# Moving the pieces of the gate weights' sums behind the MLP's first product, and two gate turns into the embedding products

## The chip, the cores and the metric

The kernel runs on one core of one Trainium2 chip. The metric is the time of one execution on the device, in microseconds. The core's engines work side by side, each on its own queue in order: TensorE (PE) multiplies, VectorE (DVE) and ScalarE (ACT) work on tiles element by element, SyncE (SP) issues most of the DMA transfers, and ScalarE's queue issues some as well. They wait for each other through semaphores.

## The reference

Two layers of a decoder trunk on 512 tokens of width 1024, all float32. Each layer is a token mixer (SSD, then HGRN2), a layer norm, an MLP with squared ReLU, a second layer norm and a gated embedding:

```python
def sq_relu_mlp(h, w1, w2):
    a = jax.nn.relu(h @ w1)
    return (a * a) @ w2
...
        h = layer_norm(DEEPNORM_ALPHA * x + mix, ln_g[i, 0], ln_b[i, 0])
        h = layer_norm(DEEPNORM_ALPHA * h + sq_relu_mlp(h, mlp_w1[i], mlp_w2[i]), ln_g[i, 1], ln_b[i, 1])
        x = h + jax.nn.sigmoid(h @ ple_w_gate[i]) * (p[i] @ ple_w_proj[i])
```

The change lies in the last two of these lines: w1 is 1024 x 4096, w2 4096 x 1024, the gate weights 1024 x 1024 and the embedding's projection 256 x 1024.

## The kernel before

**Arithmetic.** Every float32 factor is split into a high and a low part (`split`: a copy to the matmul's type on ScalarE, L114, into a `whi` tile; a subtraction on VectorE, L116, into a `wlo` tile), and `mm3` multiplies three of the four pairs (L120 to L122), 128x128 by 128x512 each. The pools of whi and wlo tiles have six slots each, which all the weights share. A slot that is written again waits for everything that read it.

**The MLP's schedule.** The hidden 4096 columns are worked on in four groups. `hidden(g)` makes a group's 8 tiles of the first product (each a T: 24 matmuls, ReLU L528, square L530); after every four of them `half_blocks` (L345 to L371) makes half of the group's seven blocks a11, a22, a12, s2, s3, s1 and s4, sums and differences of quarters, each put as a high copy (L357, ScalarE) and a low rest (L358, VectorE). The blocks s3 and s4 live in `blk` buffers, of which there are two per name, the others in `b8` buffers. `block_product` then makes the group's part of the second product in seven products p1 to p7 of 24 matmuls (each a Q), from these blocks and from sums of w2's quarters; every product is added to `acc` on VectorE (L471, or L473 the first time, L467 in the last group). The table `PERIODS` sets the order: period 0 is eight Ts, periods 1 to 3 are TTQTQTQTQTQTQTQ (the Ts of group g, the Qs of group g - 1), period 4 is seven Qs. The first Q of a period is p1 (a11).

**The gate weights' sums.** The gate's product uses the same scheme, so its weights' sums are made ahead: `sums_ahead` (L392 to L425) is a generator of 20 steps. For each of four pieces it takes one whi and one wlo tile as room for four quarters (loads L402 on SP), makes the sums (L405, L406, then L409, L410 on VectorE), and then, in two pairs, copies the high part into an `sg` tile (L417) and stores it to `pre` in memory (L418), subtracts to get the low part (L420, VectorE), and stores that (L425, issued by ScalarE). The whi and wlo slots are held until the last L425 has landed. `sg` has two buffers. The period loop takes one step after each Q of periods 1 to 3; what is left is taken at the start of period 4.

**Order.** The schedule follows the order in which the program is written, with offsets of priority, and `behind(x)` keeps what is issued within it behind the instruction x. The vector rows of the gate pieces stand behind `marks["acc"]`, the last accumulate that was written (L467, L471 or L473); the L425 stores stand behind `marks["act"]`, the last ReLU.

**Turns and embedding.** After the MLP, `turned(c)` transposes a chunk of the normed rows on TensorE (L318, into banks pt and pm) and splits it for the gate's product. turned(0) stands behind the last matmul of p3 in period 4 (c, k = 1, 3), turned(1) between proj(0, 0) and proj(1, 0), which are the first two products of the embedding (6 matmuls each).

Of the kernel before, what the change touches and what calls it, by code (L numbers as in the profile page):

```python
# [16 lines left out]
T = 512  # L17
# [15 lines left out]
SUMS = (60, 300, 300, 300)  # L33
# [8 lines left out]
def trunk(ctx: ExitStack, tc, a):  # L42
    nc = tc.nc
# [14 lines left out]
    uid, marks = [0], {}  # L58
# [5 lines left out]
    def mk(p, shape, tag, dt=F32, **kw):  # L64
        return p.tile(list(shape), dt, tag=tag, name=nm(tag), **kw)

    def f32(t):
        return t.bitcast(F32)
# [21 lines left out]
    def bank(p, tag):  # L90
        return mk(p, [P, T], tag)
# [8 lines left out]
    def behind(ins):  # L100
        return nullcontext() if ins is None else tc.issue_after(ins.ins)
# [17 lines left out]
    def mm3(out, sh, sl, mh, ml, start, stop, **kw):  # L119
        nc.tensor.matmul(out, sh, mh, start=start, stop=False, **kw)  # L120
        nc.tensor.matmul(out, sh, ml, start=False, stop=False, **kw)  # L121
        marks["pe"] = nc.tensor.matmul(out, sl, mh, start=False, stop=stop, **kw)  # L122
# [25 lines left out]
    acc = mk(accp, [P, NCH, D], "acc")  # L148
# [10 lines left out]
    with tc.high_priority(offset=FIRST):  # L159
# [7 lines left out]
        for k in range(8):  # L167
            hi, lo = (v[:, k % 4, :] for v in early[k // 4])
            x, w = slots[k][:, 0:T], slots[k][:, T:768]
# [180 lines left out]
    def half_blocks(blk, z0, z1, p):  # L350

        ks = slice(2 * p, 2 * p + 2)
        a11, a12, a21, a22 = z0[:, :, 256:], z1[:, :, 256:], z0[:, :, :256], z1[:, :, :256]

        def put(name, f):
            hi, lo = blk[name][:, 0, ks, :], blk[name][:, 1, ks, :]
            nc.scalar.copy(hi, f)  # L357
            nc.vector.tensor_sub(lo, f, f32(hi))  # L358

        put("a11", a11)  # L360
        put("a22", a22)
        nc.vector.tensor_add(a22, a21, a22)
        put("a12", a12)
        nc.vector.tensor_sub(a21, a11, a21)
        nc.vector.tensor_sub(a11, a22, a11)
        nc.vector.tensor_sub(a12, a12, a11)
        put("s2", a11)
        put("s3", a21)
        put("s1", a22)
        put("s4", a12)  # L370
# [65 lines left out]
            us.append((hi, lo))  # L436
        return us

    def block_product(w, blk, lead, first, after=None, turns=None, sums=None):

        with behind(marks.pop(("turned", 0), None) if first else None):
            t1, t2, t3, t4 = weight_sums(w, lead)
        seen = set() if first else {(i, j) for i in range(2) for j in range(2)}
        banks = {}

        def product(x, f, name, start, i, j, turns=None):
            us = [split(v) if f in (t1, t2, t3, t4) else unit(v) for v in f]
            if start:  # L450
                banks[name] = [bank(psy, "py%d" % c) if name == "x" else bank(psj, "pj") for c in range(2)]
            t = blk[x]
            for c in range(2):
                ps = banks[name][c]
                sl = slice(c * P, (c + 1) * P)
                for k in range(4):
                    hi, lo = us[k // 2]
                    ks = slice((k % 2) * 512, (k % 2 + 1) * 512)
                    w_ = hi[:, ks], lo[:, ks]
                    mm3(ps, t[:, 0, k, sl], t[:, 1, k, sl], *w_, start and k == 0, k == 3, skip_group_check=True)  # L460
                    if turns and (c, k) == (1, 3):
                        with behind(marks["pe"]):
                            turns()
                d = acc[:, 2 - 2 * i + c, j * 512 : (j + 1) * 512]
                with tc.high_priority(offset=SOON if after else 0):
                    if after and f in (w[1][0], t1, t4, w[1][1]):
                        marks["acc"] = nc.vector.tensor_tensor_reduce(  # L467
                            d, ps, d, 1.0, 0.0, ALU.add, ALU.add, sums[:, 2 - 2 * i + c, j : j + 1]
                        )
                    elif (i, j) in seen:  # L470
                        marks["acc"] = nc.vector.tensor_add(d, ps, d)  # L471
                    else:
                        marks["acc"] = nc.vector.scalar_tensor_tensor(d, d, ALPHA, ps, ALU.mult, ALU.add)  # L473
            seen.add((i, j))

        p1 = lambda: product("a11", w[0][0], "x", True, 0, 0)
        p2 = lambda: product("a12", w[1][0], "z", True, 0, 0)
        p6 = lambda: product("s2", t2, "x", False, 1, 0)
        p7 = lambda: product("s3", t3, "y", True, 1, 1)
        p5 = lambda: product("s1", t1, "x", False, 1, 1)  # L480
        p4 = lambda: product("a22", t4, "y", False, 1, 0)
        p3 = lambda: product("s4", w[1][1], "x", False, 0, 1, turns)
        for f in (p1, p7, p6, p4, p5, p2, p3) if after else (p1, p2, p6, p7, p5, p4, p3):
            f()
            if after and f is p5:
                after(0), after(1)
            if after and f is p3:
                after(2), after(3)
            yield

    def mlp_and_gate(layer, h_s, last, turns=()):

        w1, w2 = a[f"w1_{layer}"], a[f"w2_{layer}"]
        blocks = {}
# [45 lines left out]
        for g, period in enumerate(PERIODS):  # L540
            if g < 4:
                tiles = hidden(g)
            if g > 0:
                if g == 4:
                    blk, after, turned, sums, later = norm_blocks(2 * layer + 1)
                    p_s = (mk(w4, [P, 2, T], "a", F32R), mk(w4, [P, 2, T], "b", F32R))
                    praw = mk(raws, [P, 1024], "raw")
                    nc.sync.dma_start(praw, a[f"pT_{layer}"].rearrange("p k t -> p (k t)"))
                    praw = praw.rearrange("p (k t) -> p k t", k=2)
                    nc.scalar.copy(p_s[0], praw)  # L550
                    nc.vector.tensor_sub(p_s[1], praw, f32(p_s[0]))
                w = [[[w2[8 * g - 8 + 4 * i + 2 * j + u] for u in range(2)] for j in range(2)] for i in range(2)]
                products = block_product(w, blocks.pop(g - 1), SUMS[g - 1], g == 1, *((after, lambda: turned(0), sums) if g == 4 else ()))
            for op in period:
                next(tiles if op == "T" else products)
                if 0 < g < 4 and op == "Q":
                    next(ahead, None)
                if g == 4:
                    for _ in ahead:
                        pass  # L560
# [14 lines left out]

        pus, pps, held = {}, {}, {}

        def proj(c, h, parts=1):
            if h not in pus:
                pus[h] = unit(a[f"wp_{layer}"][h])  # L580
            pu = pus[h]
            pps[c, h] = []
            n = 512 // parts
            for i in range(parts):
                pp = bank(psj, "pj")[:, :n]
                for k in range(2):
                    ks = slice(k * 512 + i * n, k * 512 + (i + 1) * n)
                    mm3(pp, p_s[0][:, k, c * P : (c + 1) * P], p_s[1][:, k, c * P : (c + 1) * P], pu[0][:, ks], pu[1][:, ks], k == 0, k == 1)
                pps[c, h].append(pp)

        def product(x, f, c, ps, start, hook=()):
            cs = slice(c * P, (c + 1) * P)
            for k in range(4):
                hi, lo = f[k // 2]
                ks = slice((k % 2) * 512, (k % 2 + 1) * 512)
                mm3(ps, blk[x][:, 0, k, cs], blk[x][:, 1, k, cs], hi[:, ks], lo[:, ks], start and k == 0, k == 3, skip_group_check=True)
                for at in hook:
                    if (c, k) == at[:2]:
                        with behind(marks["pe"]):
                            turned(at[2])  # L600
# [15 lines left out]
                late.append(lambda: turn(h, c))  # L616

        two = lambda p, tag: [bank(p, tag % c if "%" in tag else tag) for c in range(2)]
        proj(0, 0)
        with behind(marks["pe"]):  # L620
            turned(1)
        proj(1, 0)
        xb = two(psy, "py%d")
        f = [unit(v) for v in wb[0][0]]
        for c in range(2):
# [3 lines left out]
        f = [unit(v) for v in wb[1][0]]  # L629
# [8 lines left out]
        f = ready(pre, 2)  # L638
# [9 lines left out]
        f = ready(pre, 1)  # L648
# [4 lines left out]
        f = ready(pre, 3)  # L653
# [5 lines left out]
        f = ready(pre, 0)  # L659
# [7 lines left out]
        f = [unit(v) for v in wb[1][1]]  # L667
# [14 lines left out]
    first = [bank(psy, "py0"), bank(psy, "py1")]  # L682
    for k in range(8):
        if k == 6:
            for i in range(8):
                for c in range(NCH):
# [4 lines left out]
                        start=i == 0,  # L691
# [3 lines left out]
        parts = [tuple(v[:, k % 4, i * P : (i + 1) * P] for v in early[k // 4]) for i in range(2)]  # L695
# [241 lines left out]
    with tc.manual_schedule(engines={mybir.EngineType.PE}):  # L937
# [8 lines left out]
        for k in range(1, 9):  # L946
            i, j = 2 * k, 2 * k + 1
# [542 lines left out]
```

## Time and profile before

| | us |
|---|---|
| median of 3 runs (1411.07 to 1411.56) | 1411.1 |
| the profiled execution | 1411.54 |
| its span, first to last instruction | 1409.8 |
| ScalarE busy in it | 777.6 |
| VectorE busy in it | 1076.0 |

The first layer's MLP runs from about 393 to 700 us of the span, the second layer's about 652 us later. Times in rows are microseconds from the start of the span. A row of the timeline gives the start, the duration, the engine, the line, the operation and the tiles (written<-read, buffer numbers left out), and in brackets the idle time of the engine before it with what ended it. A queue's name with a q (ACTq, SPq) is the engine issuing a DMA.

### The profile page before, as it was taken

The page shows a single profiled execution, that of the slowest core. Times are in us where ns is not written, and L with a number is a line of the kernel's source. Part 1 is how long each engine was busy: PE and PEld are TensorE (multiplying, and loading weights), DVE is VectorE, ACT ScalarE, POOL GpSimd, SP SyncE. Part 2 cuts the span into 40 slices and gives each one's busy share as a digit, 9 for nine tenths or more (in the row PEclk, how much of TensorE's full clock was granted, in tenths as well). Part 3 has the DMA queues.
Part 4 walks back from the last instruction along what each step waited for, and adds up shares of the span by engine and source line. Part 5 has one row for each costly group of instructions (what it writes and reads, how often), then busy time and mean ns, then how long its engine had stood idle before and what let it go on. Part 6 is the DMA issues. An engine that isn't in the chain of part 4 may idle for free.

```text
span 1409.8 us, 20492 instructions
## 1 busy us (share of the span) xinstructions
PE 1400.4 (99%) x7973; PEld 1168.9 (83%) x7973; DVE 1076.0 (76%) x1777; ACT 777.6 (55%) x1164; POOL 1.8 (0%) x11
## 2 busy tenths in 40 slices
PE   9999999999999999999999999999999999999998
PEld 7888888888988888887888888888898888888787
DVE  7997877696866878787985774776785877868986
ACT  7886666573554555545564446465454554544563
POOL 0000000000000000000000000000000000000000
PEclk9999999999999999999999999999999999999999
DMA  8423333323354646655473321222163566565364
GB/s 295 157 98 135 103 108 120 105 90 105 129 185 143 228 161 204 211 176 177 139 280 122 104 92 62 89 92 75 61 239 122 171 209 214 175 215 194 108 246 154
DMA packets 66819, 214.70 MB, mean 152 GB/s; under 512 B 7713, under 2 KB 8353, under 8 KB 66593
## 3 DMA queue, kind: packets, MB, share of 16 engines
q1 hardware_dynamic: 57504, 196.59, 41.6%
q10 hardware_dynamic: 9216, 16.78, 3.3%
q8 instruction: 63, 1.03, 0.3%
q14 instruction: 36, 0.29, 0.1%
HBM read 194.41 MB, written 18.94 MB: 151 GB/s over the span
## 4 chain that ended last, share of the span: by engine, by line
PE 96%; DMA 1%; DVE 1%; ACT 1%; issue 1%; SPq 0%; DVEq 0%; ACTq 0%
PE pj L120 25%; PE pj L122 24%; PE pj L121 24%; PE py L120 5%; PE py L122 5%; PE py L121 5%; PE py L881 1%; PE py L1147 1%; PE py L883 1%; DVE wlo L116 1%; PE pt L864 0%; DMA raw<-in_whvg 0%; DMA acc<-in_xw 0%; ACT whi L114 0%; DMA pre<-whi 0%
## 5 line engine op out<-in xcount | busy, mean ns | idle before, releaser
L116 DVE TENSOR_TENSOR wlo<-raw,whi 128x1024 fp32r<-128x1024 f32 x222 | 269.4, 1221 | 171.6 <-ACT whi L114 170.4
L114 ACT CAST whi<-raw 128x1024 fp32r<-128x1024 f32 x222 | 232.8, 1051 | 302.3 <-PE pj L121 157.5
L120 PE MATMUL pj<-b,whi 128*128 128x512 f32 (+1 forms) x1000 | 379.6, 380 | 0.0
L121 PE MATMUL pj<-b,whi 128*128 128x512 f32 (+1 forms) x1000 | 377.3, 377 | 0.0
L122 PE MATMUL pj<-b,wlo 128*128 128x512 f32 (+1 forms) x1000 | 377.3, 377 | 0.0
L122 PEld LDWEIGHTS pj<-b,wlo 128*128 128x128 f32 x1000 | 188.2, 188 | 34.8
L121 PEld LDWEIGHTS pj<-b,whi 128*128 128x128 f32 x1000 | 188.2, 188 | 34.2
L120 PEld LDWEIGHTS pj<-b,whi 128*128 128x128 f32 x1000 | 188.0, 188 | 34.1
L122 PE MATMUL pj<-whi,b 128*128 128x512 f32 x530 | 206.1, 389 | 0.0
L120 PE MATMUL pj<-whi,b 128*128 128x512 f32 x496 | 196.1, 396 | 0.0
L121 PE MATMUL pj<-wlo,b 128*128 128x512 f32 x496 | 193.2, 390 | 0.0
L114 ACT CAST whi<-r 128x1024 fp32r<-128x1024 f32 x64 | 67.2, 1053 | 96.6 <-PE pj L121 79.9
L122 PEld LDWEIGHTS pj<-whi,b 128*128 128x128 f32 x530 | 99.5, 188 | 20.7 <-DVE b L1342 0.2
L120 PEld LDWEIGHTS pj<-whi,b 128*128 128x128 f32 x496 | 93.2, 188 | 20.3 <-ACT k L1076 0.5
L121 PEld LDWEIGHTS pj<-wlo,b 128*128 128x128 f32 x496 | 93.2, 188 | 18.5
L120 PE MATMUL py<-whi,b 128*128 128x512 f32 x256 | 100.7, 393 | 3.1 <-ACT b L357 3.1
L122 PE MATMUL py<-whi,b 128*128 128x512 f32 x256 | 99.8, 390 | 0.0
L121 PE MATMUL py<-wlo,b 128*128 128x512 f32 x256 | 99.7, 389 | 0.0
L116 DVE TENSOR_TENSOR wlo<-r,whi 128x1024 fp32r<-128x1024 f32 x64 | 77.8, 1220 | 27.8 <-ACT whi L114 24.0
L120 PEld LDWEIGHTS py<-whi,b 128*128 128x128 f32 x256 | 48.0, 188 | 15.0 <-ACT b L357 3.9
L122 PEld LDWEIGHTS py<-whi,b 128*128 128x128 f32 x256 | 48.1, 188 | 10.1
L121 PEld LDWEIGHTS py<-wlo,b 128*128 128x128 f32 x256 | 48.1, 188 | 9.7
(374 smaller groups left out, 1934.1 us busy)
## 6 DMA issues: line engine op xcount, KB each, us to landing
raw<-in_w SPq DMA_DIRECT2D x112, 512.0 KB, 3.4
r<-in_w SPq DMA_DIRECT2D x64, 512.0 KB, 4.0
raw<-in_wssd SPq DMA_DIRECT2D x38, 512.0 KB, 3.6
a<-csd SPq DMA_DIRECT2D x16, 512.0 KB, 3.6
raw<-in_wso SPq DMA_DIRECT2D x16, 512.0 KB, 3.7
pre<-sg ACTq DMA_DIRECT2D x32, 256.0 KB, 3.0
whi<-pre SPq DMA_DIRECT2D x16, 512.0 KB, 5.3
wlo<-pre SPq DMA_DIRECT2D x16, 512.0 KB, 6.6
```

The costliest lines, as they stand in the source:

```text
L114: nc.scalar.copy(hi[:, :n], f)
L116: nc.vector.tensor_sub(lo[:, :n], f, f32(hi[:, :n]))
L120: nc.tensor.matmul(out, sh, mh, start=start, stop=False, **kw)
L121: nc.tensor.matmul(out, sh, ml, start=False, stop=False, **kw)
L122: marks["pe"] = nc.tensor.matmul(out, sl, mh, start=False, stop=stop, **kw)
L881: nc.tensor.matmul(yd[64 * r : 64 * r + 64, sl], xdt[:, c, r, :], m[:, r, sl], start=True, stop=c == 0)
L883: nc.tensor.matmul(yd[64 * r : 64 * r + 64, sl], pv[:, c - 1, r, :], ecs[:, r, (c - 1) * P : c * P], start=False, stop=True,)
L1147: nc.tensor.matmul(ps[r][32 * b : 32 * b + 32, base + n * c : base + n * c + n], kk[r][:, ts], moving(r, 4 * c + b), start=True, stop=True,)
```

## The change

Three edits, none of which adds or removes an instruction on TensorE or VectorE. The step of `sums_ahead` is taken after each T of periods 1 to 3 instead of each Q (24 Ts against 21 Qs). `half_blocks`' put makes its L358 the new `marks["acc"]`, so that a piece stands behind the last block made if that was written later than the last accumulate. turned(0) and turned(1) stand behind the first three matmuls of proj(0, 0) and proj(1, 0), and the `turns` parameter of `block_product` goes.

```diff
@@ half_blocks
             nc.scalar.copy(hi, f)
-            nc.vector.tensor_sub(lo, f, f32(hi))
+            marks["acc"] = nc.vector.tensor_sub(lo, f, f32(hi))
@@ block_product
-    def block_product(w, blk, lead, first, after=None, turns=None, sums=None):
+    def block_product(w, blk, lead, first, after=None, sums=None):
...
-                    if turns and (c, k) == (1, 3):
-                        with behind(marks["pe"]):
-                            turns()
...
-        p3 = lambda: product("s4", w[1][1], "x", False, 0, 1, turns)
+        p3 = lambda: product("s4", w[1][1], "x", False, 0, 1)
@@ mlp_and_gate
             for op in period:
                 next(tiles if op == "T" else products)
-                if 0 < g < 4 and op == "Q":
+                if 0 < g < 4 and op == "T":
                     next(ahead, None)
...
-        def proj(c, h, parts=1):
+        def proj(c, h, parts=1, turn=None):
...
                     mm3(pp, p_s[0][:, k, c * P : (c + 1) * P], p_s[1][:, k, c * P : (c + 1) * P], pu[0][:, ks], pu[1][:, ks], k == 0, k == 1)
+                    if turn == c and k == 0:
+                        with behind(marks["pe"]):
+                            turned(c)
...
-        proj(0, 0)
-        with behind(marks["pe"]):
-            turned(1)
-        proj(1, 0)
+        proj(0, 0, turn=0)
+        proj(1, 0, turn=1)
```

Line numbers of the changed kernel differ a little: its L468 is L471 of before, and its L525, L527, L547 and L567 are L528, L530, L550 and L570.

VectorE in the first layer, at the end of period 3 and the start of period 4, before. The two L420 are the last of the fourth gate piece; acc<-py_935 is the accumulate of p1's first half in period 4, and wlo_5646, 5678 and 5682 belong to weights of period 4's products.

```order
L420 TENSOR_TENSOR whi_5154<-whi_5154,sg_5462 128x512
L420 TENSOR_TENSOR wlo_5155<-wlo_5155,sg_5466 128x512
L116 TENSOR_TENSOR wlo_5642<-r_5578,whi_5640 128x1024
L471 TENSOR_TENSOR acc_94<-py_842_5041,acc_94 128x512
L116 TENSOR_TENSOR wlo_5646<-r_5587,whi_5644 128x1024
L116 TENSOR_TENSOR wlo_5678<-r_5581,whi_5676 128x1024
L358 TENSOR_TENSOR blk_4938<-b_5079,blk_4938 128x512
L116 TENSOR_TENSOR wlo_5682<-r_5590,whi_5680 128x1024
L358 TENSOR_TENSOR b_814_4934<-b_5393,b_814_4934 128x512
L358 TENSOR_TENSOR b_813_4933<-b_5393,b_813_4933 128x512
L362 TENSOR_TENSOR b_5393<-a_5247,b_5393 128x2x256
L471 TENSOR_TENSOR acc_94<-py_935_5612,acc_94 128x512
```

The same place after the change, from the s4 block of the first half (blk_4956<-b_5091) on; the accumulate of the previous group's py (L471 there) and four rows of the second half's blocks stand ahead of it.

```order
L358 TENSOR_TENSOR blk_4956<-b_5091,blk_4956 128x512
L420 TENSOR_TENSOR whi_4906<-whi_4906,sg_5225 128x512
L420 TENSOR_TENSOR wlo_4907<-wlo_4907,sg_5229 128x512
L116 TENSOR_TENSOR wlo_5678<-r_5581,whi_5676 128x1024
L365 TENSOR_TENSOR a_5267<-b_5405,a_5267 128x2x256
L358 TENSOR_TENSOR blk_4955<-a_5267,blk_4955 128x512
L366 TENSOR_TENSOR b_5405<-b_5405,a_5267 128x2x256
L358 TENSOR_TENSOR b_820_4954<-a_5267,b_820_4954 128x512
L116 TENSOR_TENSOR wlo_5682<-r_5590,whi_5680 128x1024
L358 TENSOR_TENSOR b_819_4953<-b_5405,b_819_4953 128x512
L358 TENSOR_TENSOR blk_4956<-b_5405,blk_4956 128x512
L468 TENSOR_TENSOR acc_94<-py_935_5612,acc_94 128x512
```

The L420 pair has moved from ahead of the previous group's last accumulates to behind the s4 block, and most of the second half's blocks now stand ahead of the accumulate of py_935. ScalarE at the same place, before:

```order
L425 DMA pre<-whi_5154 128x512
L530 ACTIVATE b_5393<-b_5393 128x1024
L425 DMA pre<-wlo_5155 128x512
L114 CAST whi_5644<-r_5587 128x1024
L114 CAST whi_5676<-r_5581 128x1024
L357 CAST blk_4938<-b_5079 128x512
L114 CAST whi_5680<-r_5590 128x1024
```

and after:

```order
L114 CAST whi_5644<-r_5587 128x1024
L357 CAST b_819_4953<-b_5405 128x512
L357 CAST blk_4956<-b_5091 128x512
L114 CAST whi_5676<-r_5581 128x1024
L357 CAST blk_4955<-a_5267 128x512
L425 DMA pre<-whi_4906 128x512
L425 DMA pre<-wlo_4907 128x512
L357 CAST b_820_4954<-a_5267 128x512
L114 CAST whi_5680<-r_5590 128x1024
```

The two stores L425 have moved from ahead of the casts into the next weights' tiles to between them; whi_5680 takes the slot of whi_4906.

VectorE at the end of period 2 of the same layer, before; acc<-py_744 is the last accumulate of group 1, the bank of which the second half of period 3's p1 takes.

```order
L116 TENSOR_TENSOR wlo_5039<-raw_5035,whi_5037 128x1024
L364 TENSOR_TENSOR a_4620<-a_4620 128x2x256
L358 TENSOR_TENSOR blk_4311<-b_4444,blk_4311 128x512
L365 TENSOR_TENSOR a_4620<-b_4766,a_4620 128x2x256
L358 TENSOR_TENSOR blk_4310<-a_4620,blk_4310 128x512
L366 TENSOR_TENSOR b_4766<-b_4766,a_4620 128x2x256
L358 TENSOR_TENSOR b_717_4309<-a_4620,b_717_4309 128x512
L358 TENSOR_TENSOR b_716_4308<-b_4766,b_716_4308 128x512
L358 TENSOR_TENSOR blk_4311<-b_4766,blk_4311 128x512
L116 TENSOR_TENSOR wlo_5085<-raw_5081,whi_5083 128x1024
L471 TENSOR_TENSOR acc_94<-py_744_4415,acc_94 128x512
```

After, from the last third of the same stretch on; L405, L406, an L116 and L365 stand ahead of these rows:

```order
L409 TENSOR_TENSOR whi_4497<-wlo_4498,whi_4497 128x512
L366 TENSOR_TENSOR b_4776<-b_4776,a_4630 128x2x256
L410 TENSOR_TENSOR wlo_4498<-wlo_4498,whi_4497 128x512
L420 TENSOR_TENSOR wlo_4498<-wlo_4498,sg_4734 128x512
L420 TENSOR_TENSOR whi_4497<-whi_4497,sg_4738 128x512
L358 TENSOR_TENSOR b_717_4311<-a_4630,b_717_4311 128x512
L358 TENSOR_TENSOR blk_4312<-a_4630,blk_4312 128x512
L358 TENSOR_TENSOR b_716_4310<-b_4776,b_716_4310 128x512
L358 TENSOR_TENSOR blk_4313<-b_4776,blk_4313 128x512
L116 TENSOR_TENSOR wlo_5097<-raw_5093,whi_5095 128x1024
L420 TENSOR_TENSOR whi_4497<-whi_4497,sg_4811 128x512
L420 TENSOR_TENSOR wlo_4498<-wlo_4498,sg_4815 128x512
```

Directly behind the last of these stands the accumulate of py_748, which is py_744 of before. The third gate piece's rows, all eight of them, have moved in ahead of it.

More of the change, by code (lines that the diff above doesn't have):

```diff
@@ L446, in block_product, with product @@
         banks = {}
-        def product(x, f, name, start, i, j, turns=None):
+        def product(x, f, name, start, i, j):
             us = [split(v) if f in (t1, t2, t3, t4) else unit(v) for v in f]
@@ L552, in mlp_and_gate @@
                 w = [[[w2[8 * g - 8 + 4 * i + 2 * j + u] for u in range(2)] for j in range(2)] for i in range(2)]
-                products = block_product(w, blocks.pop(g - 1), SUMS[g - 1], g == 1, *((after, lambda: turned(0), sums) if g == 4 else ()))
+                products = block_product(w, blocks.pop(g - 1), SUMS[g - 1], g == 1, *((after, sums) if g == 4 else ()))
             for op in period:
                 next(tiles if op == "T" else products)
-                if 0 < g < 4 and op == "Q":
+                if 0 < g < 4 and op == "T":
                     next(ahead, None)
```

## The prediction

> **What bounds the kernel now.** The page first: how much of the span is TensorE, and what the chain that ended last is made of.
>
> ```profile
> span 1409.8 us, 20492 instructions
> ...
> PE 1400.4 (99%) x7973; PEld 1168.9 (83%) x7973; DVE 1076.0 (76%) x1777; ACT 777.6 (55%) x1164; POOL 1.8 (0%) x11
> ...
> PE 96%; DMA 1%; DVE 1%; ACT 1%; issue 1%; SPq 0%; DVEq 0%; ACTq 0%
> ```
>
> TensorE is idle for 1409.8 - 1400.4 = 9.4 us of the span. The change adds and removes no matmul, so nothing but these 9.4 us, or new pauses, can move the time. The view of the waits says what ended the idle time of TensorE (total, how often, longest):
>
> ```profile
> PE py L120 <- ACT b L357: 3.1, 2, 1.8
> PE pm L155 <- DVE y L152: 1.1, 1, 1.1
> PE py L120 <- ACT whi L174: 0.7, 2, 0.5
> PE pt L318 <- ACT b L324: 0.3, 1, 0.3
> PE pm L570 <- DVE acc L612: 0.2, 1, 0.2
> ```
>
> The second and third rows belong to the program's start; 9.4 less the five rows' 5.4 is its first load and its tail. The change reaches the first row, the fourth, and at most the last: 3.1 + 0.3 + 0.2 = 3.6 us, 0.25% of the time. About 0.2%, 2.8 us, is what a measurement of this kernel can tell from no change. The windows of 20 us put the 3.1 us in two places, one for each layer's MLP (TensorE's busy time is the second number):
>
> ```profile
> 660.00:680.00 20.00, 18.77 (x81) 14.41 (x80) 19.70 (x26) 12.56 (x17) 0.00 (x0) 1.00 0.15 53
> 1300.00:1320.00 20.00, 18.16 (x80) 14.75 (x79) 13.98 (x18) 11.20 (x14) 0.00 (x0) 1.00 0.46 160
> ```
>
> 20.00 - 18.77 = 1.23 and 20.00 - 18.16 = 1.84 us: 3.07 in all. Both lie at the start of period 4, where p1 accumulates its first half. The timeline of the first of them (start, duration; PE, DVE, ACT and its DMA queue apart):
>
> ```profile
> 665.08 0.39 PE L122 MATMUL pj<-whi,blk 128*128 128x512 f32 x1
> 666.70 0.47 PE L120 MATMUL py<-whi,b 128*128 128x512 f32 x1 [1.23 <-ACT b L357]
> ...
> 657.35 0.69 DVE L471 TENSOR_TENSOR acc<-py,acc 128x512 f32<-128x512 f32 x1 [0.63 <-PE py L122]
> 660.04 2.36 DVE L116 TENSOR_TENSOR wlo<-r,whi 128x1024 fp32r<-128x1024 f32 x2 [2.00 <-PE py L122]
> 662.32 0.69 DVE L358 TENSOR_TENSOR blk<-b,blk 128x512 fp32r<-128x512 f32 x1
> 662.92 1.22 DVE L116 TENSOR_TENSOR wlo<-r,whi 128x1024 fp32r<-128x1024 f32 x1
> 664.06 1.29 DVE L358 TENSOR_TENSOR b<-b,b 128x512 fp32r<-128x512 f32 x2
> 665.87 0.68 DVE L471 TENSOR_TENSOR acc<-py,acc 128x512 f32<-128x512 f32 x1
> ...
> 654.86 0.33 ACTq L425 DMA_DIRECT2D pre<-whi  x1
> 658.96 2.00 ACT L114 CAST whi<-r 128x1024 fp32r<-128x1024 f32 x2 [1.92 <-DMA pre<-whi]
> ```
>
> Matmuls start 0.23 us apart, so the next one was due at 665.31. It reuses the bank py0 and needs the L471 at 665.87, done at 666.55 (the view names L357, which ended within 0.1 us of it). That L471 stands on VectorE behind L116s whose casts waited for a whi slot, and that slot was still being stored by the last gate piece (L425): issued 654.86, released 658.96, 4.1 us. The second layer shows the same store longer in the way:
>
> ```profile
> 1319.27 0.47 PE L120 MATMUL py<-whi,b 128*128 128x512 f32 x1 [1.84 <-ACT b L357]
> 1319.57 0.40 PE L121 MATMUL py<-wlo,b 128*128 128x512 f32 x1
> 1319.80 0.39 PE L122 MATMUL py<-whi,b 128*128 128x512 f32 x1
> ...
> 1307.44 0.33 ACTq L425 DMA_DIRECT2D pre<-whi  x1
> 1311.53 2.00 ACT L114 CAST whi<-r 128x1024 fp32r<-128x1024 f32 x2 [2.54 <-DMA pre<-whi]
> ```
>
> **The change part by part.** *The pieces of the gate sums.* 20 steps per layer stood behind 21 Qs of periods 1 to 3 and stand behind the first 20 of 24 Ts: the same instructions, SP's loads and ACT's stores among them, at other times. What decides is the edit in half_blocks: `marks["acc"]` is now also the last of its L358s, and a piece issued after a T waits for it. So the last pair of L420s, whose casts are long done, stands behind the last L358 (s4) of period 3's first half. That L358 waits for its blk buffer, which p3 of the products reads until p1 begins:
>
> ```profile
> 659.64 0.39 PE L122 MATMUL py<-whi,blk 128*128 128x512 f32 x1
> 659.87 0.39 PE L120 MATMUL py<-whi,b 128*128 128x512 f32 x1
> ```
>
> VectorE after the change, by the order of its rows and the pitches above (0.60 us for 512 columns, 662.32 to 662.92; 1.14 for 1024, 662.92 to 664.06): the L471 of 657.35; two L358, L362 and an L116 from 657.95; L364 at 660.89; the s4 L358 at 661.49 (its copy on ACT ends about 661.05, so it doesn't wait); L420s at 662.09 and 662.69. ScalarE, in order, issues the store of whi then: 662.09 + 0.68 = 662.8, **8 us later than the 654.86 of before**. VectorE goes on: L116 663.29, L365, L358, L366, L358 up to 666.83, where the L116 of the last s2 weight comes. Its cast writes into the gate tile's whi slot, so it waits for that store. How long a store takes to land:
>
> ```profile
> raw<-in_w SPq DMA_DIRECT2D x2, 512.0 KB, 3.6
> pre<-whi ACTq DMA_DIRECT2D x1, 256.0 KB, 4.0
> b<-in_ln SPq DMA_DIRECT2D x1, 512.0 KB, 3.4
> DMA to landing us min/median/max: 2.0/4.1/7.4
> ```
>
> The first two rows are the loads and that store in the window 650 to 662, the third a load after it, the fourth all transfers of `pre`. The 512 KB load of b is freed by the same s4 L358, so it travels at the same time; before, the store had two 512 KB weight loads in its window and took 4.1. I take 4.1 and keep 2.0 and 7.4 as ends. Then the cast starts at 662.8 + 4.1 = 666.9 and ends at 667.95 (2.00 / 2 each, plus 0.05), the L116 runs 668.0 to 669.1, two L358 follow, and the L471 of py0 runs from 670.3 to 671.0. TensorE needs 0.15 more (666.55 to 666.70): 671.15. In the new order its wait comes 12 matmuls later than before, because a piece of p7 goes ahead: 665.31 + 12 x 0.227 = 668.03. **The pause is 671.15 - 668.03 = 3.1 us.** With the store landing at once, VectorE's own queue (666.83 + 1.14 + 2 x 0.60 + 0.68 + 0.15 = 670.0) still leaves 2.0; this floor holds up to a landing of 3.0 us, and from there every microsecond counts in full. One more accumulate, of py1, stands two L116s and a row later: 670.3 + 0.60 + 2 x 1.14 + 0.68 = 673.9, + 0.15 against 671.15 + 12 x 0.227 = 673.9: another 0.15. In the second layer every row stands 652 us later in the same order, and the store is again tied to the s4 L358, which hangs on TensorE; so I take the same 3.1 + 0.15 there. Terms: 2 x 3.25 - 3.07 = **+3.4 us**.
>
> The landing by rule: the Trainium skill, "DMA: Bandwidth & Descriptors", section "Anatomy of one DMA — SWDGE (gpsimd) path", gives about 2.0 us plus the bytes at 436 GB/s. That is an estimate of 2.6 us for 256 KB, under the 3.0 of the floor, and the sum would be 2 x 2.15 - 3.07 = +1.2 us. The trace disagrees, with 4.0 for the very store beside two loads, and the measured number stays in the sum.
>
> *The end of period 2.* The same edit puts the second L420 pair of the third gate tile ahead of an accumulate that p1 of period 3 needs. The rows there:
>
> ```profile
> 585.29 0.68 DVE L471 TENSOR_TENSOR acc<-py,acc 128x512 f32<-128x512 f32 x1
> ...
> 591.87 0.39 PE L120 MATMUL py<-whi,b 128*128 128x512 f32 x1
> ...
> pre<-sg ACTq DMA_DIRECT2D x32, 256.0 KB, 3.0
> ```
>
> Before, this L471 ended at 585.97, 5.9 us early. Now one L116 and eight 512-column rows (L405, L406, L409, L410, four L420) that stood elsewhere come ahead of it, 1.14 + 8 x 0.60 = 5.9 us, so it ends at 591.9: on time, or 0.1 late. The last two L420s also wait for casts into sg buffers whose stores must land first; at the median of 3.0 us they don't add to this, at 5 us they make it 1.4 late. I take nothing; a loss of 1 us in each layer goes into the range. At the end of period 1 the same bunch has over 4 us of room.
>
> *The turns.* turned(0) and turned(1) move 3 matmuls later, inside proj's products; 9 matmuls of proj stand between them and the next turn's pt as before:
>
> ```profile
> 703.51 0.66 PE L318 MATMUL pt<-cst,acc 128*128 128x128 f32 x4 [0.26 <-ACT b L324]
> ```
>
> I count this 0.26 at nothing: bounds -0.3 (it goes) to +0.7 (3 matmuls of cover, 3 x 0.23, are lost at the first turn). *Loads.* No row of TensorE's waits names a weight load in the MLP; loads that move cost nothing while that holds.
>
> The sum on the profiled execution, 1411.54 us (1.7 around the span): 1411.5 + 3.4 = 1414.9. The median of the runs shown is 1411.1, so 1411.1 + 3.4 = **1414.5 us**.
>
> **The rivals.**
> *The stores land in under 3 us.* For it: the 2.0 us minimum, and the queue is quieter than at 655. Against: both stores in the trace took 4.1. Each pause is then the floor, 2.0 + 0.15: +1.2, 1412.3 us, no change.
> *Faster: the old pauses go.* TensorE's wait for the py0 accumulate moved 2.7 us later, from 665.31 to 668.03. If the last L420 pair ran before the s4 L358 could hold it, VectorE would reach the accumulate in time, and both pauses vanish: 1411.1 - 3.1 = 1408.0 us. It decides at the store's issue: the accumulate must end by 667.9, so the cast must be over by 664.8 and the store must land by 663.7. An issue at 662.8 is too late even at 2.0 us, and the order ties it there; only a blk buffer freed 1 us earlier or more would do, and TensorE reads that buffer until 659.9.
> *Slower still: a slow start after a long pause.* At the kernel's start, and after the 1.23 pause by a little (0.47 against 0.39), matmuls behind a pause stand further apart:
>
> ```profile
> 8.69 0.51 PE L120 MATMUL py<-b,whi 128*128 128x512 f32 x1 [0.19 <-ACT whi L174]
> 9.11 0.50 PE L121 MATMUL py<-b,whi 128*128 128x512 f32 x1
> ```
>
> That is 0.42 instead of 0.23. If it held for as long as the pause (3.1 / 0.42 = 7.4 matmuls, 0.19 each), each layer pays 1.4 more: 1417.3 us. Against it: after 1.84 us the starts were 0.23 apart (1319.57, 1319.80), at a granted clock of 1.00. The Trainium skill, "TensorE: Matmul & The Clock Gate", section "What's actually happening", says that an idle window of about 3.4 us halves the clock until a busy one has passed. No run here shows a pause that long in the middle of work; by that rule 3.1 us is just short of it.
> *The change does nothing here*, because what waits at period 4 is the same chain with another name: 1411.1 us.
>
> **How the numbers follow.** Forecast 0.50, slow start 0.07, quick landing 0.30, nothing 0.04, old pauses gone 0.09. Slower by over 0.2% (above 1413.9): 0.50 + 0.07 = 0.57. Within 0.2%: 0.34. Faster: 0.09. The range takes in the floor, nothing at all, and the slow start or a second place that costs 1 us a layer: 1411.0 to 1417.5. Left out are the old pauses gone (0.09) and landings near 7.4 (3.3 more each, 1421).
>
> **What would show it.** Right: L420 of the last gate tile near 662 and its L425 near 662.8; TensorE pausing 3 us near 668 and again in the second layer, released by L471; a window 660 to 680 with about 16.8 busy. Short stores: pauses of 2.0 with no DMA in the chain. Wrong: a cast of the last s2 weight before 665, no pause at 668, or a pause at 591.9 of over 1 us, which I have put at nothing.

## The result, and the profile after

The changed kernel takes 1416.2 us (median of 9 runs, 1414.2 to 1418.4) against 1412.0 for the kernel before in the same comparison: a ratio of 1.0029, 95% interval 1.002 to 1.0038. On the record stood +3.4 us: 1414.5 for the median, 1414.9 for a profiled execution; the profiled one took 1414.78. In a second comparison (below), 1415.2 against 1412.4, the ratio was 1.0018 (1.0008 to 1.0029). The change makes the kernel slower by 0.2 to 0.3%.

The page and the view of TensorE's waits after the change:

```profile
span 1413.0 us, 20501 instructions
PE 1401.9 (99%) x7973; PEld 1171.0 (83%) x7973; DVE 1077.0 (76%) x1777; ACT 775.0 (55%) x1164; POOL 1.8 (0%) x11
PE py L120 <- DVE acc L468: 6.0, 2, 3.0
PE pm L155 <- DVE y L152: 1.1, 1, 1.1
```

Where the waits had 3.1 us on two pauses, they now have 6.0 on two, and the releaser is named as the accumulate itself. The rows for L318 and L570 are gone. But TensorE is also *busy* for 1.5 us longer, with the same 7973 matmuls. The windows show one cause (the third number from the end is the granted clock):

```profile
660.00:680.00 20.00, 16.97 (x67) 13.31 (x66) 17.02 (x24) 9.68 (x13) 0.00 (x0) 0.91 0.24 79
1320.00:1340.00 20.00, 17.05 (x74) 13.36 (x73) 17.17 (x23) 10.09 (x11) 0.00 (x0) 1.00 0.23 85
```

Behind the first pause the clock was not full: 0.91 on the mean of 20 us. The timeline there (VectorE, then ScalarE and its queue, then TensorE):

```profile
661.84 0.69 DVE L358 TENSOR_TENSOR blk<-b,blk 128x512 fp32r<-128x512 f32 x1
662.44 0.68 DVE L420 TENSOR_TENSOR whi<-whi,sg 128x512 fp32r<-128x512 f32 x1
668.63 1.22 DVE L116 TENSOR_TENSOR wlo<-r,whi 128x1024 fp32r<-128x1024 f32 x1 [1.35 <-ACT whi L114]
670.98 0.68 DVE L468 TENSOR_TENSOR acc<-py,acc 128x512 f32<-128x512 f32 x1
...
663.16 0.33 ACTq L425 DMA_DIRECT2D pre<-whi  x1
667.55 1.05 ACT L114 CAST whi<-r 128x1024 fp32r<-128x1024 f32 x1 [1.43 <-DMA pre<-whi]
...
668.30 0.39 PE L122 MATMUL pj<-whi,blk 128*128 128x512 f32 x1
671.72 0.50 PE L120 MATMUL py<-whi,b 128*128 128x512 f32 x1 [3.03 <-DVE acc L468]
672.06 0.40 PE L121 MATMUL py<-wlo,b 128*128 128x512 f32 x1
672.80 0.63 PE L121 MATMUL py<-wlo,b 128*128 128x512 f32 x1
673.22 0.63 PE L122 MATMUL py<-whi,b 128*128 128x512 f32 x1
675.78 0.54 PE L122 MATMUL py<-whi,b 128*128 128x512 f32 x1
676.16 0.39 PE L120 MATMUL py<-whi,b 128*128 128x512 f32 x1
```

Read from the top: the s4 block, the L420 right behind it, the store at 663.16, the cast that waits for it until 667.55, the L116, the accumulate, TensorE. From 672.80 matmuls start 0.43 us apart instead of 0.23, up to 676.16. These 3.36 us hold 8 matmuls, which need 8 x 0.227 = 1.8 at full rate: 1.5 us lost. Windows of 1 us show the clock itself:

```profile
672.00:673.00 1.00, 1.00 (x5) 0.78 (x5) 1.00 (x2) 0.00 (x0) 0.00 (x0) 0.84 0.00 0
673.00:674.00 1.00, 1.00 (x3) 0.79 (x3) 1.00 (x2) 0.00 (x0) 0.00 (x0) 0.50 0.00 0
675.00:676.00 1.00, 1.00 (x4) 0.81 (x3) 1.00 (x2) 0.00 (x0) 0.00 (x0) 0.50 0.00 0
```

It is halved. In the second layer of this execution it was not:

```profile
1325.92 0.50 PE L120 MATMUL py<-whi,b 128*128 128x512 f32 x1 [2.95 <-DVE acc L468]
1326.25 0.39 PE L121 MATMUL py<-wlo,b 128*128 128x512 f32 x1
1326.48 0.40 PE L122 MATMUL py<-whi,b 128*128 128x512 f32 x1
```

So the change doubled two pauses, as forecast, and on top of that a stretch at half clock followed one of the two pauses of 3 us. The experiments ask two things: which edit makes the pauses, and whether the half clock is a price of idling.

### The profile page after: what moved, and what is told of

It reads as the page before. It is cut to its first block, busy times and chain, and to the rows that moved or that the text cites. A ratio compares the mean times of both kernels' runs of the same rounds, so it can differ in the third digit from the quotient of the medians.

```text
span 1413.0 us, 20501 instructions
## 1 busy us (share of the span) xinstructions
PE 1401.9 (99%) x7973; PEld 1171.0 (83%) x7973; DVE 1077.0 (76%) x1777; ACT 775.0 (55%) x1164; POOL 1.8 (0%) x11
## 4 chain that ended last, share of the span: by engine, by line
PE 98%; DVE 1%; DMA 1%; ACT 0%; issue 0%; DVEq 0%; ACTq 0%
PE pj L120 25%; PE pj L122 24%; PE pj L121 24%; PE py L120 5%; PE py L121 5%; PE py L122 5%; PE py L879 1%; PE py L1145 1%; PE py L881 1%; DMA pre<-whi 1%; PE pt L862 0%; PE pt L226 0%; PE pm L155 0%; DVE b L358 0%; PE pt L822 0%; PE pt L1314 0%
## 5 line engine op out<-in xcount | busy, mean ns | idle before, releaser
L116 DVE TENSOR_TENSOR wlo<-raw,whi 128x1024 fp32r<-128x1024 f32 x222 | 269.8, 1222 | 180.5 <-ACT whi L114 176.2
L116 DVE TENSOR_TENSOR wlo<-r,whi 128x1024 fp32r<-128x1024 f32 x64 | 77.8, 1221 | 28.2 <-ACT whi L114 27.9
```

The lines of the kernel that those rows point to most:

```text
L116: nc.vector.tensor_sub(lo[:, :n], f, f32(hi[:, :n]))
```

## The experiments

### One edit undone: no mark in put

```diff
-            marks["acc"] = nc.vector.tensor_sub(lo, f, f32(hi))
+            nc.vector.tensor_sub(lo, f, f32(hi))
```

In `sums_ahead` the pieces stand behind `marks.get("acc")`, since the first ones come before any accumulate.

> The changed kernel with one edit undone: half_blocks' put no longer sets the mark, so a gate piece stands behind the last accumulate alone. Theory: the mark is what ties the last L420 pair to the s4 block, and with it the L425 stores and the slot of the last s2 weight. Then the pair runs some 50 us earlier, VectorE reaches the py0 accumulate at 666.8 to 667.5, TensorE needs it at about 668.0, and both pauses go: 6.0 us of pauses and the 1.5 us at half clock less than the profile of the change, a span near 1405.5 and a time near 1407.3 us, about 4 us under before. Rival (it is the steps behind T as such, or the turns, and VectorE is simply full there): the pauses stay at 2 to 3 us each and the time within 1 us of the change.

Measured: **1405.3 us** (4 runs, 1405.2 to 1405.8), ratio to before 0.9948 (0.9932 to 0.9965), span 1403.8. The span is 1.7 us below the 1405.5 expected: it is 9.2 us under that of the change, of which the pauses and the half clock make 7.5; the other 1.7 no row names. The waits of TensorE have a single row left, the one at the start of the program, and the rows at the place are those foreseen: the accumulate in time, TensorE without a gap at 668.04.

```profile
PE pm L155 <- DVE y L152: 1.0, 1, 1.0
...
666.79 1.28 DVE L468 TENSOR_TENSOR acc<-py,acc 128x512 f32<-128x512 f32 x2
...
667.81 0.39 PE L122 MATMUL pj<-whi,blk 128*128 128x512 f32 x1
668.04 0.62 PE L120 MATMUL py<-whi,b 128*128 128x512 f32 x2
```

The mark in put is what makes the pauses, and without it the steps behind T remove even those of before.

### The step ahead of the T, with the mark

```diff
+                if 0 < g < 4 and op == "T":
+                    next(ahead, None)
                 next(tiles if op == "T" else products)
-                if 0 < g < 4 and op == "T":
-                    next(ahead, None)
```

> The changed kernel, mark and all, but with the step taken ahead of the T instead of behind it, so that a piece that falls on the fourth T is written ahead of that T's half_blocks. Theory (what costs is only that the last pair is written right behind the s4 block): the pair stands some 50 us earlier, as without the mark, no pauses, no half clock, 1405 to 1406 us. Rival (the mark delays pieces elsewhere, so that other accumulates come late): pauses of 0.5 us or more at the ends of periods 1 or 2 and a time over 1407.

Measured: 1405.3 us (1404.9 to 1405.4), ratio 0.9951 (0.9935 to 0.9967), no wait of TensorE but the start's. The mark by itself is harmless: what costs is that step 20 falls on the fourth T of period 3, whose half_blocks has just been written, so that the mark is the s4 block. One statement earlier, it is not. This kernel, the one without the mark and the next one, all at 1405, beat both the kernel before and the changed one.

### The second edit alone: steps behind T, turns and put as before

Against the kernel before, again with `marks.get`:

```diff
-                if 0 < g < 4 and op == "Q":
+                if 0 < g < 4 and op == "T":
```

> Only the second edit: steps behind T, no mark in put, and the two turns where before has them (turned(0) behind p3's last matmul, turned(1) between the two products). Theory: no pauses at the start of period 4, and the waits of the transposes of before, 0.3 and 0.2 us or a little more, are there again: 0.3 to 1.0 us above the kernel with the turns moved too (1405.3), so 1405.6 to 1406.3. Rival (the turns carry a good part of the gain): 1407 or more, with idle time of TensorE of 1 us or more at L318 or L570.

Measured: 1405.4 us (1405.0 to 1405.7), ratio 0.9952 (0.9936 to 0.9968). The waits of the transposes that I expected back are not there: the turns are worth nothing measurable once the pauses are gone.

### The third edit alone: the turns

Against the changed kernel:

```diff
-            marks["acc"] = nc.vector.tensor_sub(lo, f, f32(hi))
+            nc.vector.tensor_sub(lo, f, f32(hi))
...
-                if 0 < g < 4 and op == "T":
+                if 0 < g < 4 and op == "Q":
```

> Only the third edit: the steps stand behind Q again and put sets no mark, the two turns stay inside the embedding's products. Theory: the two pauses of before come back, 1.2 and 1.8 us, and the waits of the transposes (L318 0.3, L570 0.2 in before) are gone: 0.5 us under before, 1410.6 on before's 1411.1, which can't be told from no change; the rows of waits decide. Rival (the turns carry part of the loss): the time is 1 us or more above before, and a wait for L318 or L324 shows.

Measured: 1412.0 us (10 runs, 1409.3 to 1413.8), ratio 0.9996 (0.9986 to 1.0005): no change, as expected, and the rows for L318 and L570 are gone. But the pauses in its profile are not those of before:

```profile
PE py L120 <- ACT b L357: 5.6, 2, 3.1
...
653.35 1.05 ACT L114 CAST whi<-raw 128x1024 fp32r<-128x1024 f32 x1 [1.67 <-DMA raw<-in_w]
656.29 0.33 ACTq L425 DMA_DIRECT2D pre<-whi  x1
...
668.33 0.47 PE L120 MATMUL py<-whi,b 128*128 128x512 f32 x1 [3.12 <-ACT b L357]
```

The instructions at this place stand in the order of before, yet the store is issued at 656.29 instead of 654.86, because VectorE's L420 pair stood behind the L116 of a weight that arrived late. So in this order the length of the pauses depends on when weights land, and the 1.23 and 1.84 us of one execution of before need not be all there was: no second execution of before has a profile. The 9 to 22 runs of before in these comparisons have medians of 1412.0 to 1412.5, not 1411.1, and reach from 1409.6 to 1416.8.

### The store taken out of the chain

```diff
-                        lows.append((dst[n, u, 1][:, cs], f32(x)))
+                        low = hi if (u, h, n) in ((1, 1, 0), (1, 1, 3)) else x
+                        lows.append((dst[n, u, 1][:, cs], f32(low)))
```

> The changed kernel, but the last two L425 of each layer's last gate piece store the sg tiles (the high parts) in place of the low parts, so that the whi and wlo slots are free as soon as VectorE has read them; the low parts of that piece are left out of the gate's weights. The stores' number and size stay. Theory: the cast of the last s2 weight no longer waits for a landing and each pause falls from 3.0 to VectorE's own queue, 2.0 us at most; since the L116 moves ahead of four short rows it may come to 1.9 to 2.1. Time 2 us under the change without the half clock, 3.5 with it. Rival (the landing is beside the point, VectorE's queue alone sets the pause): pauses stay at 3.0.

Measured: 1410.1 us (10 runs, 1409.4 to 1411.8), ratio 0.9981 (0.9972 to 0.999); no cast waits for a store at these two places any more.

```profile
PE py L120 <- DVE acc L469: 1.8, 2, 0.9
PE pj L122 <- DVE blk L358: 1.2, 2, 0.6
```

Each layer's pause is 0.9 + 0.6 = 1.5 us, in two pieces. I expected 1.9 to 2.1; the freed L116 goes ahead of the s3 piece that p7 needs, which makes a small wait of its own, and the accumulate is earlier for it. About half of the 3 us is the store's landing, the other half VectorE's queue behind the s4 block. The landing alone is therefore not the cause; the place of the pair is, as the kernels without pauses show. The time is 6.1 us under the change's 1416.2, where I had expected 2 to 3.5: the shorter pauses are 3.0 of it, and the mean clock of 0.9997 instead of 0.9978 is about 2.7 more, an estimate (0.0019 x 1410).

### A longer pause

One multiplication of the acc slice by 1 on VectorE ahead of the accumulate, behind the last put:

```diff
@@ half_blocks
-            marks["acc"] = nc.vector.tensor_sub(lo, f, f32(hi))
+            marks["acc"] = marks["put"] = nc.vector.tensor_sub(lo, f, f32(hi))
@@ block_product
+                if after and x == "a11" and c == 0:
+                    with behind(marks["put"]), tc.high_priority(offset=SOON):
+                        for _ in range(1):
+                            nc.vector.tensor_scalar_mul(d, d, 1.0)
```

> The changed kernel with a multiplication by 1 of the acc slice put ahead of the py0 accumulate in period 4 (one 512-column row on VectorE), ahead of which the order then puts one more L116: the pause grows by 0.6 + 1.14, to about 4.7 us in each layer. It asks what the length of the pause does to TensorE's clock. Theory A (the granted clock is halved for some 3.4 us when most of a window of that length was idle): it is halved behind nearly every one of the two pauses in every execution; the time is 3.5 + 1.5 us or so above the change's profile, near 1420, the mean clock 0.997 to 0.998 in every run. Theory B (a whole window must be idle): some 4 pauses in 10, mean clocks scattered from 1.000 to 0.998. Theory C (the fall has nothing to do with the pause): as often as in the change, and 3.5 us for the pauses alone.

Measured: 1419.8 us (4 runs, 1419.4 to 1421.2), ratio 1.0053 (1.0038 to 1.0068), mean clocks 0.995 to 0.998 in every run.

```profile
PE py L120 <- DVE acc L472: 9.2, 2, 4.7
660.00:680.00 20.00, 15.31 (x55) 11.87 (x54) 15.85 (x22) 8.10 (x12) 0.00 (x0) 0.83 0.25 79
1320.00:1340.00 20.00, 15.51 (x58) 11.96 (x57) 16.08 (x22) 7.14 (x8) 0.00 (x0) 0.83 0.24 79
```

TensorE's rows behind the pauses, the first and the last of the slow stretch in each layer:

```profile
673.38 0.79 PE L120 MATMUL py<-whi,b 128*128 128x512 f32 x1 [4.69 <-DVE acc L472]
679.09 0.49 PE L122 MATMUL py<-whi,b 128*128 128x512 f32 x1
...
1330.32 0.80 PE L120 MATMUL py<-whi,b 128*128 128x512 f32 x1 [4.49 <-DVE acc L472]
1334.32 0.55 PE L121 MATMUL py<-wlo,b 128*128 128x512 f32 x1
```

The clock was at half behind both pauses of this execution, and no run's mean clock is above 0.998, which is Theory A, though the mean clock fell further than it said (0.997 to 0.998). Theory C (no link with the pause) is out. So is Theory B (a window of 3.4 us must be idle as a whole): the changed kernel's clock fell behind a pause of 3.03.

### The same pauses, filled with matmuls

Matmuls that nobody reads, on TensorE right ahead of the one that waits: 12 or 8 in the changed kernel, 18 in the one with the longer pause. With 8:

```diff
+            if after and x == "s2":
+                idle = bank(psm, "pm")
+                with behind(marks["pe"]):
+                    for _ in range(8):
+                        nc.tensor.matmul(idle, blk["a11"][:, 0, 0, 0:P], blk["a11"][:, 0, 0:2, :].rearrange("p a t -> p (a t)"), start=True, stop=True)
```

> The changed kernel with 12 matmuls of 128x512 that nobody reads put on TensorE, from the a11 block into the bank pm, right ahead of the matmul that waits for the py0 accumulate: 12 x 0.227 = 2.7 us of work inside the pause of 3.0. Theory (the half clock is the price of idling, on top of the pause): the pause that is left is 0.3 us, the waiting matmul starts when it did, and the clock is never halved: mean clock 1.000 in every run, the times close together near 1413, 2.5 to 3.5 us under the median of the change. Rival (the half clock has another cause, or the extra matmuls cost time): mean clocks of 0.995 to 0.999 stay, and the time is that of the change or above.

Measured: 1416.1 us (10 runs, 1415.5 to 1417.3), ratio 1.0029 (1.0019 to 1.0038). The clock recovered to a mean of 0.9993, but the time did not fall: a miss. In its profile the store of the second layer landed after 6.3 us, and 2.2 us of pause were left behind the filling:

```profile
PE py L120 <- DVE acc L473: 3.2, 4, 2.2
...
pre<-whi ACTq DMA_DIRECT2D x1, 256.0 KB, 6.3
```

That could be a cost of the filling or an accident of this program's transfers (not of one execution alone: the ten runs lie within 1.8 us); the next run took fewer matmuls, beside the changed kernel itself on the same chip.

> The changed kernel itself, on the chip of the two runs beside it, so that their times and clocks have one to stand against: 1416 us, mean clocks from 0.995 to 0.999, pauses of 3.0 us, a store that lands in 4.0 to 4.5 us.

Measured: 1415.2 us (9 runs, 1413.8 to 1418.4), pauses 3.0 and 3.1, mean clock 0.9976, stores 4.3 and 4.4 us.

> As the kernel with 12 unread matmuls ahead of the waiting one, but with 8 (1.8 us of the pause of 3.0). With 12 the clock stayed near 1.000 and the time still did not fall; its profile had a store of 6.3 us in the second layer. Theory A (that store was slow by where other transfers happened to fall, and the half clock is a cost of idling): with other transfers beside it the store lands in 4.0 to 4.5, the pause left is 1.2 us, clocks are 0.999 to 1.000, and the time is 2 to 3 us under the changed kernel. Theory B (the extra matmuls themselves make the store or VectorE slower): the store takes over 5 us again in the second layer and the time equals that of the changed kernel.

Measured: **1412.6 us** (10 runs, 1412.3 to 1413.2), ratio 1.0002 (0.9993 to 1.0011), mean clock 0.9999, store 4.3 and 4.5 us.

```profile
PE py L120 <- DVE acc L473: 2.4, 2, 1.3
660.00:680.00 20.00, 18.86 (x82) 14.84 (x81) 18.53 (x24) 9.85 (x13) 0.00 (x0) 1.00 0.24 79
```

The pause left is 1.2 to 1.3 us, which with the filling of 8 x 0.227 = 1.8 makes the 3.0 of the changed kernel: the accumulate came no sooner. Still the kernel is 2.6 us faster than the changed one beside it, by doing useless work, and its runs lie within 0.9 us instead of 4.6. That is the cost of the half clock, apart from that of the pause.

> The kernel whose pause was 4.7 us, with 18 unread matmuls (4.1 us) ahead of the waiting one. Without them it took 1419.8 us at mean clocks of 0.995 to 0.998, and in its profile matmuls ran at half the rate for 6.0 and 4.3 us. Theory A (half clock by idling): clocks 0.999 to 1.000 and 4 us or so less, near 1416. Theory B (the filling saves nothing): 1419 to 1420.

Measured: 1416.6 us (8 runs, 1416.0 to 1417.4), ratio 1.0028 (1.0018 to 1.0039), mean clock 0.9995: 3.2 us less than the same pauses unfilled (those on another chip, where before had 1412.5 against 1412.4 here). Theory A again. What made the store of the kernel with 12 matmuls slow is open; with 8 and with 18 it was not.

## Why the prediction was right, and where its steps were off

**The pauses, as predicted.** The stretch of VectorE ran by the predicted steps. It was 0.35 us late up to the store, mostly because period 4 began at 660.17 instead of 659.87, and 0.7 us late from the cast on, because the store took 0.3 longer (4.39 against 4.1 from issue to cast): s4 block 661.84 (predicted 661.49), L420 662.44 (662.09), store 663.16 (662.8), cast 667.55 (666.9), accumulate 670.98 (670.3). Counted as the prediction counted it, from the start that was due (668.30 + 0.227 = 668.53) to the start that was, the pause is 671.72 - 668.53 = 3.19 against 3.12. Undoing the mark removes it, so the reason is shown, not only the size. Of the rivals, "the stores land in under 3 us" fell with the 4.3 us that the view of transfers gives, "the change does nothing" with the two pauses.

**The second accumulate** (0.15 us in each layer) cost nothing that shows: no second wait stands behind either pause.

**The end of period 2** held at "on time, or 0.1 late". The accumulate ends at 591.98, and the matmul that waits for it, due at 591.69 + 0.227 = 591.92, starts 0.11 late:

```profile
591.29 0.69 DVE L468 TENSOR_TENSOR acc<-py,acc 128x512 f32<-128x512 f32 x1
...
591.69 0.39 PE L122 MATMUL py<-whi,b 128*128 128x512 f32 x1
592.03 0.50 PE L120 MATMUL py<-whi,b 128*128 128x512 f32 x1
```

**The half clock was a rival with 0.07, and it happens in most runs.** This is the step that failed: I took a pause of 3.1 us as just short of what halves the clock, and weighed the case by the 1.84 us pause that had left it alone. The mean clock of 18 runs of the changed kernel is 0.9977, never above 0.999: at most 1415 x 0.0023 = 3.3 us lost in a mean run, by estimate. At most, because this mean counts the program's end too, where the clock falls once the matmuls are done and costs nothing: in the profiles that is up to 0.0007, and the kernel with the step ahead of the T has a mean of 0.999 without any pause. So 0.998 or less, which 11 of the 18 runs have, shows a fall in the work; of the seven with 0.999 the two profiled ones do. The price, 1.4 us a pause, came out right (1.5 measured) by luck: I took it from rows at the kernel's start, where the granted clock is 1.00. The Trainium skill's rule ("TensorE: Matmul & The Clock Gate", section "What's actually happening") speaks of an idle window of about 3.4 us. The stretch at half clock did last 3.4 us, but pauses of 3.0 and 3.1 us, shorter than the window, were enough; those of before, 1.23 and 1.84, were not in the profiled execution.

What decides here is how a pause lies on a fixed grid. The stretches of half clock within the work last 3.41 or 6.83 us, and the full ones between two falls are whole multiples of the same 3.413 (737.28 = 216 x 3.413 in the changed kernel, from 676.09 on). Windows on this grid (the first two numbers are length and TensorE's busy time), at the two pauses of the changed kernel:

```profile
669.27:672.68 3.41, 0.96 (x4) 0.83 (x5) 3.41 (x5) 2.69 (x3) 0.00 (x0) 1.00 0.00 0
672.68:676.09 3.41, 3.41 (x10) 2.65 (x9) 3.41 (x5) 0.00 (x0) 0.00 (x0) 0.50 0.00 0
1321.21:1324.63 3.42, 1.76 (x8) 1.13 (x6) 2.15 (x4) 2.88 (x4) 0.00 (x0) 1.00 0.05 18
1324.63:1328.04 3.41, 2.12 (x9) 1.78 (x10) 3.41 (x5) 1.53 (x2) 0.00 (x0) 1.00 0.02 5
```

The pause of 3.03 us fell for the most part into one window and left it 0.96 us of work; the one of 2.95 was split over two, with 1.76 and 2.12. In the twelve traces every window at full clock with 1.42 us of work or less is followed by half clock, and every one with 1.60 or more by full clock. So a pause of 3 us is charged or not by where it begins, which would make the runs scatter.

**The base was taken too low.** The three runs shown had a median of 1411.1, and the profiled one full clock; over 22 runs before has a median of 1412.4 and a mean clock of 0.9989, at most 1.5 us lost (part of it may be the end of the program, as above). The kernel with the turns alone shows how: in the same order the pause reached 3.1 us when a weight landed late, and its clock fell. So half clock was missing on both sides of my sum. That +3.4 came out near the measured +2.8 to +4.2 is right for the pauses and in part luck: in the profiled executions the half clock (+1.5), which I left out, and the terms below (-1.2) nearly cancel.

**What was counted at nothing.** In the profiled executions the two pauses cost +2.9 us and the half clock +1.5, together 4.4, but the span grew by 3.2 (1413.0 against 1409.8). The turns' waits for L318 and L570, which are gone, are 0.5 of the difference. The other 0.7 us no row names, and they stay open; the row for L174 at the program's start, 0.7 before, is gone too, but both executions show 131 matmuls in the first 20 us.

**"Old pauses gone"** was the rival on the faster side, at 1408. I tied it to the s4 block's buffer and held it impossible in this order, rightly; but it takes only one statement's place to have it, and then it is worth more than I said, 1405.3. In the profiled executions, both without half clock in the work, that is 6.0 us of span (1409.8 to 1403.8), of which before's pauses are 3.1 and the turns' waits 0.5; the rest is not traced.

## What to carry to other kernels

When pieces of side work are hung behind "the last" instruction of some kind, look at which one that is at the place where each piece is written: a piece that was ready 50 us earlier was tied to a block that waits for a buffer, with a store and a shared slot behind it. Where one engine is busy 99% of the time, a pause of 3 us costs it more than 3 us if its clock falls, so remove pauses rather than balance them, and read the clock in windows behind each pause. TensorE's busy time alone doesn't show it: for the same matmuls it was 1400.4 us before and 1398.7 without the mark, both at full clock in the work. A baseline whose pauses hang on when loads land is not one number: take more than three runs of it, and read the clock of each.

## What the runs showed of the hardware

A pause of 3.03 us between matmuls led to a granted clock of 0.50 that began about 1 us after work had resumed (at 671.72; the window 672 to 673 has 0.84) and lasted some 3.4 us. With pauses of 4.7 and 4.5 the resumed work was slow from its first matmul, for about 6 us in one layer and 4.3 in the other. Two pauses of 2.95 and 3.03 us in one execution had different outcomes, by where they lay on a grid of 3.413 us: windows of it with at most 1.42 us of work were followed by half clock, those with 1.60 or more were not. And the mean clock of the same program ranged from 0.995 to 0.999 from run to run. The 256 KB store of the last gate piece landed after 4.0 to 4.5 us in the profiles in which a cast of period 4 waits for it, but for 6.3 us in one layer of one of them.
